# Re-cutting fourteen loads against ScalarE, and twelve unread products ahead of TensorE's last ones

## The chip, the cores and the metric

One core of one Trainium2 chip. The metric is the device time of one execution in microseconds (us), as a median over executions. A "span" is the same execution in the profile, from the first to the last instruction, some 1.8 us shorter than the device time. The experiments ran in four groups on four chips; each group has its own runs of the kernel before, and times are compared inside a group. A run counts as slow when it lies over 1.5% above the fastest of its kernel in the group; medians below are of all runs, ratios of fast runs alone.

## The reference

A cross-entropy loss per row: for 256 rows of 32000 float32 logits, the log of the sum of exponentials, less the logit that the label names.

```python
log_probs = logits - np.max(logits, axis=-1, keepdims=True)
log_probs = log_probs - np.log(np.sum(np.exp(log_probs), axis=-1, keepdims=True))
return np.array([-log_probs[i, labels[i]] for i in range(batch)])
```

## The kernel before

Each of the 128 partitions holds two rows, 64000 columns in one line. They arrive in 14 loads (numbered 0 to 13), all issued by SyncE on one queue. ScalarE runs one exp over each load, which also sums it (two where a load crosses from the first row into the second). The logit of the label is gathered, exp(-g) goes on the diagonal of a matrix, and TensorE multiplies the row sums with it, so that the log of the result is the loss.

```python
CHUNKS = [
    1024, 14528, 13376, 8960, 7168, 5056, 3584,
    2816, 2176, 1536, 1280, 1024, 768, 704,
]
# ... (cut)
for i in range(done, last):
    exps(i)                                   # ScalarE: exp of load i, sum into parts
    if i == turn:                             # first row complete
        nc.vector.reduce_sum(out=sums[:, 0:1], in_=parts[0][:, :], ...)
        nc.tensor.matmul(lane[0][:, :], sums[:, 0:1], diag[0][:, :], start=True, stop=True)
    if i == turn + 1:
        log_row(0)                            # ScalarE: Ln of the first row's products
nc.vector.reduce_sum(out=sums[:, 1:2], in_=parts[1][:, :], ...)
nc.tensor.matmul(lane[1][:, :], sums[:, 1:2], diag[1][:, :], start=True, stop=False)
exps(last)                                    # load 13
nc.tensor.matmul(lane[1][:, :], s_last[:, :], diag[1][:, :], start=False, stop=True)
log_row(1)
nc.sync.dma_start(out=out..., in_=res...)
```

The last three lines are a chain: nothing can start before the last exp's sum is read. Below, "the sums' product" is the first of the two products of row 1, "the last product" the second.

The softmax here doesn't subtract the row's maximum and nothing guards it: scores larger than these inputs give would overflow.

Of the kernel before, what the change touches and what calls it, by code (L numbers as in the profile page):

```python
# [9 lines left out]
P = 128  # L10
ROWS = 2
F32 = mybir.dt.float32
# [3 lines left out]


CHUNKS = [
    1024, 14528, 13376, 8960, 7168, 5056, 3584,
    2816, 2176, 1536, 1280, 1024, 768, 704,  # L20
]
SLOTS = [0, 1, 2, 3, 4, 5, 2]
TAIL = len(SLOTS)
TAIL_SLOT = 1


def begin_first_load_before_barrier(nc):
# [15 lines left out]
@with_exitstack  # L43
def kernel(
    ctx: ExitStack,
    tc: tile.TileContext,
    logits: bass.AP,
    labels: bass.AP,
    out: bass.AP,
):  # L50
    nc = tc.nc
    nc.at_finalize(begin_first_load_before_barrier)
    B, C = logits.shape
    assert B == P * ROWS and sum(CHUNKS) == ROWS * C


    flat = logits.rearrange("(p r) c -> p (r c)", r=ROWS)


    pieces = []  # L60
    starts = []
    at = 0
    for n in CHUNKS:
        starts.append(at)
        cuts = [at] + [c for c in range(C, ROWS * C, C) if at < c < at + n] + [at + n]
        pieces.append([(a, b, a // C) for a, b in zip(cuts, cuts[1:])])
        at += n
    last = len(CHUNKS) - 1

    turn = next(i for i in range(len(CHUNKS)) if starts[i] + CHUNKS[i] >= C)  # L70

    big = ctx.enter_context(tc.tile_pool(name="big", bufs=1))
    small = ctx.enter_context(tc.tile_pool(name="small", bufs=1))
    psum = ctx.enter_context(tc.tile_pool(name="psum", bufs=1, space=bass.MemoryType.PSUM))

    width = {}
    for i, s in enumerate(SLOTS):
        width[s] = max(width.get(s, 0), CHUNKS[i])
    tiles = []
    for i, s in enumerate(SLOTS):  # L80
        tiles.append((big.tile([P, width[s]], F32, name=f"x{i}", tag=f"slot{s}"), starts[i]))
    tail = big.tile([P, width[TAIL_SLOT]], F32, name="x_tail", tag=f"slot{TAIL_SLOT}")
    assert sum(CHUNKS[TAIL:]) <= width[TAIL_SLOT]
    tiles += [(tail, starts[TAIL])] * (len(CHUNKS) - TAIL)

    n_of = [sum(1 for ps in pieces[:-1] for q in ps if q[2] == r) for r in range(ROWS)]
    parts = [small.tile([P, n_of[r]], F32, name=f"parts{r}") for r in range(ROWS)]
    s_last = small.tile([P, 1], F32, name="s_last")
    res = small.tile([1, ROWS * P], F32, name="res")
    sums = small.tile([P, ROWS], F32, name="sums")  # L90
    ident = small.tile([P, P], F32, name="ident")
    diag = [small.tile([P, P], F32, name=f"diag{r}") for r in range(ROWS)]
    lane = [psum.tile([1, P], F32, name=f"lane{r}") for r in range(ROWS)]
    lbl = small.tile([P, 2 * ROWS], I32, name="lbl")
    idx = small.tile([P, ROWS], I32, name="idx")
    g = small.tile([P, ROWS], F32, name="g")
    eg = small.tile([P, ROWS], F32, name="eg")

    nc.scalar.preload_act_table_set("natural_log_exp_and_others")  # L99

    lbl_words = dataclasses.replace(
        labels.tensor, shape=[labels.tensor.shape[0] * 2], dtype=I32
    )

    def load(i):
        t, base = tiles[i]
        a, b = starts[i], starts[i] + CHUNKS[i]
        nc.sync.dma_start(out=t[:, a - base:b - base], in_=flat[:, a:b])  # L108

    seen = [0] * ROWS  # L110

    def exps(i):
        t, base = tiles[i]
        for a, b, r in pieces[i]:
            if i == last:
                acc = s_last[:, :]
            else:
                acc = parts[r][:, seen[r]:seen[r] + 1]
                seen[r] += 1
            nc.scalar.activation(  # L120
                out=t[:, a - base:b - base],
                in_=t[:, a - base:b - base],
                func=AF.Exp,
                accum_out=acc,
            )

    def log_row(r):
        nc.scalar.activation(  # L128
            out=res[0:1, r:ROWS * P:ROWS], in_=lane[r][:, :], func=AF.Ln
        )  # L130

    with tc.manual_schedule():
        first = len(set(SLOTS))
        for i in range(first):
            load(i)

        nc.scalar.dma_start(
            out=lbl[:, :], in_=bass.AP(tensor=lbl_words, offset=0, ap=[[2 * ROWS, P], [1, 2 * ROWS]])
        )
        nc.gpsimd.iota(out=idx[:, :], pattern=[[C, ROWS]], base=0, channel_multiplier=ROWS * C)  # L140
        make_identity(nc, ident[:, :])
        nc.gpsimd.tensor_add(out=idx[:, :], in0=idx[:, :], in1=lbl[:, 0:2 * ROWS:2])  # L142
        for r in range(ROWS):
            nc.gpsimd.indirect_dma_start(  # L144
                out=g[:, r:r + 1],
                out_offset=None,
                in_=logits[:, :],
                in_offset=bass.IndirectOffsetOnAxis(ap=idx[:, r:r + 1], axis=1),
            )


        done = 0
        for i in range(first, len(CHUNKS)):
            slot = SLOTS[i] if i < TAIL else TAIL_SLOT
            while done <= SLOTS[:first].index(slot):
                exps(done)
                done += 1
            load(i)
        nc.scalar.activation(out=eg[:, :], in_=g[:, :], func=AF.Exp, scale=-1.0)  # L159
        for r in range(ROWS):  # L160
            nc.vector.tensor_scalar_mul(diag[r][:, :], ident[:, :], eg[:, r:r + 1])  # L161
        for i in range(done, last):
            exps(i)
            if i == turn:
                nc.vector.reduce_sum(out=sums[:, 0:1], in_=parts[0][:, :], axis=mybir.AxisListType.X)  # L165
                nc.tensor.matmul(lane[0][:, :], sums[:, 0:1], diag[0][:, :], start=True, stop=True)  # L166
            if i == turn + 1:
                log_row(0)
        nc.vector.reduce_sum(out=sums[:, 1:2], in_=parts[1][:, :], axis=mybir.AxisListType.X)  # L169
        nc.tensor.matmul(lane[1][:, :], sums[:, 1:2], diag[1][:, :], start=True, stop=False)  # L170
        exps(last)
        nc.tensor.matmul(lane[1][:, :], s_last[:, :], diag[1][:, :], start=False, stop=True)  # L172
        log_row(1)
        nc.sync.dma_start(
            out=out.rearrange("(a n) -> a n", a=2), in_=res[0:1, :].rearrange("o (a n) -> o a n", a=2)
        )
# [30 lines left out]
```

## Time and profile before

| | before |
|---|---|
| device time, median of 4 runs (lowest to highest) | 84.88 us (84.86 to 84.90) |
| span of the profiled run | 83.03 us |
| ScalarE busy, share of the span | 58.2 us, 70% |
| mean DMA rate | 395 GB/s |
| last load landed / its exp began / its sum was read | 78.95 / 79.17 / 80.04 us |
| ScalarE's wait for the last product | 0.68 us |

"Landed" is when the sixteenth of the sixteen increments of a load's semaphore comes in the trace's landing records. Where the page of the profile gives the same fact, it is the issue's start plus its time to landing.

These are lines of part 5 of the page of the kernel before. The columns are: line, engine, operation, tiles, shapes and count; then busy us and mean ns of one; then the idle time just before the group and what ended it.

```profile
L120 ACT ACTIVATE x<-x 128x1024 f32<-128x1024 f32 (+7 forms) x8 | 46.3, 5786 | 21.3 <-DMA x<-in_logits_dram 21.3
L120 ACT ACTIVATE x_tail<-x_tail 128x2816 f32<-128x2816 f32 (+6 forms) x7 | 9.9, 1412 | 0.0
...
L172 PE MATMUL lane<-diag,s_last 128*1 128x128 f32 x2 | 0.6, 398 | 0.0
```

ScalarE's 21.3 us of idleness lies wholly before the exps of the first loads; the seven tail loads have none. And one product of 128 columns of float32 appears here as two passes of about 398 ns, which overlap: together they last 0.59 us.

### The profile page before, as it was taken

To read this page: it belongs to the slowest core of one execution; us is meant where nothing else is said; L and a number is where in the kernel's file an instruction comes from. 1 tells how busy PE (TensorE), PEld (TensorE's weight loads), DVE (VectorE), ACT (ScalarE), POOL (GpSimd) and SP (SyncE) were. 2 spreads that over 40 slices of the span, in tenths; PEclk is the share of its full clock that TensorE was granted. 3 is DMA by queue.
4 is the path that set the end of the run, shared out by engine and by line. 5 is a ranking of instruction groups with operands and counts; after the bars stand their busy time and mean duration, and the time that the engine had idled before them with its cause. 6 is when DMAs were issued, how large, how long until landed. Compare 5 with 4: busy or idle time off the path is not lost.

```text
span 83.0 us, 126 instructions
## 1 busy us (share of the span) xinstructions
PE 1.7 (2%) x6; PEld 0.3 (0%) x6; DVE 0.8 (1%) x4; ACT 58.2 (70%) x34; POOL 3.0 (4%) x10
## 2 busy tenths in 40 slices
PE   0000000000000000000000002000000000000050
PEld 0000000000000000000000000000000000000000
DVE  0000000000000000000000020000000000000000
ACT  6230000000899999029999999999999999999960
POOL 3000000000640000000000000000000000000000
DMA  4999999999999999979989799999999999999600
GB/s 87 614 448 448 448 448 448 448 448 413 412 412 413 412 413 412 412 328 501 449 380 535 307 401 428 442 451 390 458 411 414 431 434 408 400 415 405 262 0 0
DMA packets 2226, 32.77 MB, mean 395 GB/s; under 512 B 433, under 2 KB 434, under 8 KB 1202
## 3 DMA queue, kind: packets, MB, share of 16 engines
q1 hardware_dynamic: 2018, 32.77, 93.0%
q10 hardware_dynamic: 144, 0.00, 0.1%
q0 software_dynamic: 64, 0.00, 0.1%
HBM read 32.77 MB, written 0.00 MB: 395 GB/s over the span
## 4 chain that ended last, share of the span: by engine, by line
DMA 43%; ACT 37%; issue 14%; PE 1%; SPq 0%; DVE 0%
DMA x<-in_logits_dram 43%; ACT x L120 26%; ACT x_tail L120 11%; PE lane L172 1%; PE lane L170 1%; ACT res L128 1%; SPq L108 0%; DVE sums L169 0%; ACT eg L159 0%
## 5 line engine op out<-in xcount | busy, mean ns | idle before, releaser
L120 ACT ACTIVATE x<-x 128x1024 f32<-128x1024 f32 (+7 forms) x8 | 46.3, 5786 | 21.3 <-DMA x<-in_logits_dram 21.3
L120 ACT ACTIVATE x_tail<-x_tail 128x2816 f32<-128x2816 f32 (+6 forms) x7 | 9.9, 1412 | 0.0
L144 POOL DMA_INDIRECT g<-in_logits_dram,idx x2 | 2.1, 1037 | 0.6 <-issue 0.3
L99 ACT ACT_TABLE_LOAD x1 | 1.3, 1283 | 0.8 <-PEq L191 0.8
L166 PE MATMUL lane<-diag,sums 128*1 128x128 f32 x2 | 0.6, 397 | 51.4 <-DVE sums L165 51.4
L120 ACT ACTIVATION_READ_ACCUMULATOR x<-x 128x1 f32 x8 | 1.5, 186 | 0.0
L120 ACT ACTIVATION_READ_ACCUMULATOR x_tail<-x_tail 128x1 f32 x7 | 1.3, 185 | 0.0
L170 PE MATMUL lane<-diag,sums 128*1 128x128 f32 x2 | 0.6, 397 | 27.5 <-DVE sums L169 27.5
L128 ACT ACTIVATE res<-lane 1x128 f32<-1x128 f32 x2 | 0.5, 266 | 0.7 <-PE lane L172 0.7
L161 DVE TENSOR_SCALAR diag<-ident,eg 128x128 f32<-128x128 f32 x2 | 0.5, 285 | 48.5 <-ACT eg L159 48.5
L142 POOL TENSOR_TENSOR idx<-idx,lbl 128x2 int32<-128x2 int32 x1 | 0.2, 193 | 19.6 <-DMA lbl<-in_labels_dram 19.6
L172 PE MATMUL lane<-diag,s_last 128*1 128x128 f32 x2 | 0.6, 398 | 0.0
L169 DVE TENSOR_REDUCE sums<-parts 128x1 f32<-128x10 f32 x1 | 0.2, 164 | 27.9 <-ACT x_tail L120 27.9
masks.py:199 POOL TENSOR_SCALAR_AFFINE_SELECT ident<-ident 128x128 f32<-128x128 f32 x1 | 0.3, 292 | 0.1
L166 PEld LDWEIGHTS lane<-diag,sums 128*1 128x1 f32 x2 | 0.1, 80 | 51.4 <-DVE sums L165 51.4
masks.py:197 POOL MEMSET ident<- 128x128 f32 x1 | 0.2, 194 | 0.0
L159 ACT ACTIVATE eg<-g 128x2 f32<-128x2 f32 x1 | 0.2, 187 | 0.0
L165 DVE TENSOR_REDUCE sums<-parts 128x1 f32<-128x4 f32 x1 | 0.2, 157 | 2.2 <-ACT x L120 2.2
L170 PEld LDWEIGHTS lane<-diag,sums 128*1 128x1 f32 x2 | 0.1, 80 | 28.0 <-DVE sums L169 28.0
L140 POOL IOTA idx<- 128x2 int32 x1 | 0.1, 120 | 0.5 <-POOLq L191 0.5
L191 POOL MEMSET const-uint8-127<- 128x1 uint8 x1 | 0.1, 118 | 0.0
L191 POOL MEMSET const-bfloat16-1.0<- 128x1 bf16 x1 | 0.1, 112 | 0.0
(3 smaller groups left out, 0.3 us busy)
## 6 DMA issues: line engine op xcount, KB each, us to landing
x<-in_logits_dram SPq DMA_DIRECT2D x1, 7264.0 KB, 20.1
x<-in_logits_dram SPq DMA_DIRECT2D x1, 6688.0 KB, 35.7
x<-in_logits_dram SPq DMA_DIRECT2D x1, 4480.0 KB, 45.8
x<-in_logits_dram SPq DMA_DIRECT2D x1, 3584.0 KB, 53.9
x<-in_logits_dram SPq DMA_DIRECT2D x1, 2528.0 KB, 59.3
x<-in_logits_dram SPq DMA_DIRECT2D x1, 1792.0 KB
x_tail<-in_logits_dram SPq DMA_DIRECT2D x1, 1408.0 KB, 21.0
x_tail<-in_logits_dram SPq DMA_DIRECT2D x1, 1088.0 KB, 23.1
```

Of the source, the lines that this page charges most:

```text
L99: nc.scalar.preload_act_table_set("natural_log_exp_and_others")
L120: nc.scalar.activation(out=t[:, a - base:b - base], in_=t[:, a - base:b - base], func=AF.Exp, accum_out=acc,)
L128: nc.scalar.activation(out=res[0:1, r:ROWS * P:ROWS], in_=lane[r][:, :], func=AF.Ln)
L142: nc.gpsimd.tensor_add(out=idx[:, :], in0=idx[:, :], in1=lbl[:, 0:2 * ROWS:2])
L144: nc.gpsimd.indirect_dma_start(out=g[:, r:r + 1], out_offset=None, in_=logits[:, :], in_offset=bass.IndirectOffsetOnAxis(ap=idx[:, r:r + 1 ...
L159: nc.scalar.activation(out=eg[:, :], in_=g[:, :], func=AF.Exp, scale=-1.0)
L161: nc.vector.tensor_scalar_mul(diag[r][:, :], ident[:, :], eg[:, r:r + 1])
L165: nc.vector.reduce_sum(out=sums[:, 0:1], in_=parts[0][:, :], axis=mybir.AxisListType.X)
L166: nc.tensor.matmul(lane[0][:, :], sums[:, 0:1], diag[0][:, :], start=True, stop=True)
L169: nc.vector.reduce_sum(out=sums[:, 1:2], in_=parts[1][:, :], axis=mybir.AxisListType.X)
L170: nc.tensor.matmul(lane[1][:, :], sums[:, 1:2], diag[1][:, :], start=True, stop=False)
L172: nc.tensor.matmul(lane[1][:, :], s_last[:, :], diag[1][:, :], start=False, stop=True)
```

## The change

The intent is two-fold. The loads are cut anew, so that ScalarE, which in the profile of before works a column off faster than the DMA brings it (0.83 ns, from 12309 ns for 14528 columns and 772 for 704, against 1.19, from 15.92 us between landings for 13376 columns), has some slack in each step. And TensorE, idle for 27.5 us since the first row's products, is given twelve products whose result nobody reads, so that its clock is up when the last two products come. That this would raise it was an assumption; the result below shows it, with passes 109 to 110 ns apart in place of 213 to 214.

```diff
 CHUNKS = [
-    1024, 14528, 13376, 8960, 7168, 5056, 3584,
-    2816, 2176, 1536, 1280, 1024, 768, 704,
+    1024, 15104, 12672, 8960, 7136, 4992, 3872,
+    2848, 2144, 1600, 1216, 992, 800, 640,
 ]
+WARM_FROM = 8
+WARM = 12
...
+    warm = psum.tile([1, P], F32, name="warm")
...
             if i == turn + 1:
                 log_row(0)
+            if i == WARM_FROM:
+                col = parts[1][:, seen[1] - 1:seen[1]]
+                for _ in range(WARM):
+                    nc.tensor.matmul(warm[:, :], col, diag[0][:, :], start=True, stop=True)
```

The products read the sum of load 8, so that they can't begin before it is there.

## The prediction

Its sum was 84.87 less 0.18 for the sizes and 0.21 for the products, 84.48. The 0.18 is worked out from the profile of before. The 0.21 is its author's estimate: that a risen clock brings the product from 0.59 to 0.38 us was not shown by that profile. The upper figure for a risen clock, 84.51, holds a charge of 0.03 us for loads that start off 256 B.

> **What bounds the kernel now.** I read the chain that ended last first, then the loads' times to landing, then the last five microseconds instruction by instruction.
>
> The busy shares and the chain:
>
> ```profile
> PE 1.7 (2%) x6; PEld 0.3 (0%) x6; DVE 0.8 (1%) x4; ACT 58.2 (70%) x34; POOL 3.0 (4%) x10
> DMA 43%; ACT 37%; issue 14%; PE 1%; SPq 0%; DVE 0%
> ```
>
> Two things share the span. The DMA moves 32.77 MB (its row of tenths reads 9 nearly throughout), and ScalarE computes exp over the same 64000 columns. The chain in order of time shows the hand-over:
>
> ```profile
> 1.19 35.68 DMA x<-in_logits_dram
> 36.87 0.02 issue
> 36.90 0.03 ACT x L120
> ```
>
> Until 36.87 us the chain is the DMA, landing loads 0, 1 and 2; from 36.90 it is ScalarE. So the sum that sets the end today is the landing of load 2, then all the exp of loads 2 to 13 without a gap, then a tail. The same shows in ScalarE's wait on the DMA, 3 times and never after load 2:
>
> ```profile
> L120 ACT ACTIVATE x<-x 128x13376 f32<-128x13376 f32 x1 | 11.3, 11349 | 3.5 <-DMA x<-in_logits_dram 3.5
> L120 ACT ACTIVATE x_tail<-x_tail 128x704 f32<-128x704 f32 x1 | 0.8, 772 | 0.0
> ```
>
> How near the DMA runs behind is the question that decides this change. A load's landing is its issue's start plus its time to landing:
>
> ```profile
> x_tail<-in_logits_dram SPq DMA_DIRECT2D x1, 352.0 KB, 16.9
> ```
>
> The SyncE timeline puts that last issue at 62.04, so it lands at about 78.95. ScalarE starts on it at 79.17, which is 0.22 late. The landing records of the trace (sixteenth increment of each load's semaphore) give for loads 3 to 13: 47.50, 56.00, 62.02, 66.32, 69.71, 72.34, 74.23, 75.82, 77.09, 78.08, 78.95. The exps start at 48.34, 56.17, 62.49, 66.89, 70.06, 72.59, 74.59, 76.06, 77.31, 78.34, 79.17. ScalarE is thus 0.17 to 0.84 us behind each landing. It is the bound, but only by that much; if it were earlier, the DMA would be.
>
> The tail:
>
> ```profile
> 79.17 0.77 ACT L120 ACTIVATE x_tail<-x_tail 128x704 f32<-128x704 f32 x1
> 79.30 0.16 DVE L169 TENSOR_REDUCE sums<-parts 128x1 f32<-128x10 f32 x1 [27.93 <-ACT x_tail L120]
> 79.51 0.59 PE L170 MATMUL lane<-diag,sums 128*1 128x128 f32 x2 [27.50 <-DVE sums L169]
> 79.85 0.19 ACT L120 ACTIVATION_READ_ACCUMULATOR x_tail<-x_tail 128x1 f32 x1
> 80.09 0.59 PE L172 MATMUL lane<-diag,s_last 128*1 128x128 f32 x2
> 80.71 0.27 ACT L128 ACTIVATE res<-lane 1x128 f32<-1x128 f32 x1 [0.68 <-PE lane L172]
> 81.01 0.32 SPq L174 DMA_DIRECT2D out_dram<-res  x1
> ```
>
> The last accumulator read ends at 80.04, one product of two passes fills 0.59, ScalarE waits 0.68 for it, then Ln and the store, about 2.3 us that the change leaves alone.
>
> [...] 704 columns took 772 ns, 14528 took 12309. With the accumulator read I find start to start 0.833 n + 0.183 us (2816 columns: 70.06 to 72.59, 2.53).
>
> [...] TensorE here idles 27.5 us before its tail products[...]. The trace has only modelled ends, 374 ns for the first pass, 0.59 for both: 214 ns between the two ends[...]. The profile's granted clock says 1.00 throughout[...].
>
> [...] All starts of before are multiples of 64 columns (256 B)[...].
>
> **The change part by part.** *Sizes.* Same 64000 columns, same 14 loads, same 15 exp pieces, so bytes, descriptors and instruction counts stand. The DMA's end should stay at 78.95: it runs saturated, and a load costs about 1.19 ns a column between landings (load 1 to 2: 15.92 us for 13376 columns) with a little per load on top. I interpolate the new landings on the old ones by cumulative column. Loads 1 to 13 then land at 21.64, 36.72, 47.35, 55.81, 61.75, 66.40, 69.83, 72.42, 74.39, 75.90, 77.13, 78.16, 78.95.
>
> Now ScalarE against these, with 0.025 us from landing to start. Load 2 starts at 36.74, 0.15 earlier, and has 704 columns less, 0.59 us. It ends at 47.49, and the exp of the gathered labels follows to 47.59. Load 3 in its two pieces (3200 and 5760 columns) ends at 55.42. Load 4 lands only at 55.81, so ScalarE waits 0.42: the bound changes to the DMA here. Load 4 runs from 55.84 to 61.97, the first row's Ln takes 0.16, load 5 starts at 62.12, load 6 at 66.47, load 7 at 69.88. From there each starts within 0.1 us of its landing: 72.44, 74.41, 75.93, 77.16, 78.18, and the last at 79.03, against 79.17 (the same arithmetic run on the old sizes gives 79.14, a check to 0.03). Last start: 0.11 earlier by model against model. Last piece: 64 columns fewer, 0.05. Model against model the last accumulator read ends 0.16 earlier; against the measured 80.04 it is 79.84, 0.20. I take **0.18 us** gained.
>
> *Products.* Twelve products are added after load 8's exp, which ends at 74.4 and whose accumulator is read by 74.50. Each is two passes at 214 ns while cold, 0.43 us: twelve are 5.1 us, 74.55 to 79.67 if the clock never rises. [...] The sums' product L170 is ready when load 12's accumulator (79.12), the reduction (0.16) and two hand-overs are done, at 79.36. [...] cold ones delay L170 by 0.3. The last product L172 can start 0.05 after the last accumulator read, 79.89. [...] 0.59 becomes 0.38, **0.21 us** gained on the path. ScalarE's wait would fall from 0.68 to 0.47. The products wait for ScalarE, not the reverse, nothing reads their PSUM tile, and 10240 tail columns fit the slot of 15104: no new wait on ScalarE or the loads.
>
> *Sum:* 0.18 + 0.21 = 0.39; 84.87 − 0.39 = 84.48.
>
> **The rivals.** *The clock does not rise in time.* [...] If cold, the warm-up ends at 79.67, L170 runs to 80.10, and L172 starts there, where it started before (80.09): the earlier ScalarE is given back too, and the time is 84.87. That is the largest uncertainty; I give the rise in time 65%.
>
> *The sizes lose at the DMA.* Loads 5, 6, 8 and 12 of the new set start on 128 B, not on 256. [...]
>
> *ScalarE stays the bound.* From load 2 on it has 576 columns less (load 1 took them while ScalarE waited anyway), 0.48 us, and starts 0.15 earlier. Then all 0.63 us would come through, 84.03 with the clock. Against it stand the landings: the slack was 0.17 at load 4 and 0.22 at the last, and a faster ScalarE can't pass them.
>
> *The products disturb the tail.* Were a pass longer in a stream than 214 ns (each also loads weights, 80 ns in the trace, begun beside the pass before), the twelve could run to 80 or beyond and cost up to 1 us. The starts of two weight loads 3 ns apart in L172 speak against it.
>
> **Range and chances.** Clock risen (65%): 84.48 to 84.51, give or take 0.08. Not risen: 84.80 to 84.90, little changed. Most weight is at the first, so I predict 84.5 us, with 84.35 to 84.86 to hold it 8 times in 10. Two per cent is 1.7 us; nothing I found gains or loses that, so faster 0.01, within 2% 0.98, slower 0.01.
>
> **What would show it.** The step of sizes is right if ScalarE waits some 0.4 us for the DMA at 7136 columns and for some small loads after, and starts the last load near 79.0; wrong if the last load lands later than 78.97 or ScalarE never waits after load 2. The step of products is right if the later of the 24 passes are about half as far apart as the first and ScalarE's wait before the last Ln is 0.45 to 0.50; wrong if it stays 0.68, or if L170 starts only when the twelve are done.

## The result, and the profile after

| | before | changed |
|---|---|---|
| device time, median of 4 runs (lowest to highest) | 84.88 (84.86 to 84.90) | 84.41 (84.30 to 84.60) |
| span of the profiled run | 83.03 | 82.55 |
| load 2 landed, its exp began | 36.87, 36.90 | 36.70, 36.72 |
| last load landed, its exp began | 78.95, 79.17 | 78.71, 78.95 |
| last sum read | 80.04 | 79.76 |
| ScalarE's wait for the last product | 0.68 | 0.47 |

The ratio is 0.9947 (95% interval 0.9927 to 0.9966). Ratios here are the mean time of one kernel's fast runs over that of the other's of the same rounds, so not quite the ratio of the medians. In this group the change is faster by half a per cent, clear of noise and far under 2%. Two later groups repeat the pair on other chips, with more scatter: there the ratio is 0.9954 with an interval that holds 1, and 1.0018.

Part 5 of the page of the changed kernel, the groups that answer to those of before:

```profile
L124 ACT ACTIVATE x<-x 128x1024 f32<-128x1024 f32 (+7 forms) x8 | 46.4, 5794 | 20.9 <-DMA x<-in_logits_dram 20.9
L124 ACT ACTIVATE x_tail<-x_tail 128x2848 f32<-128x2848 f32 (+6 forms) x7 | 9.8, 1404 | 0.0
L176 PE MATMUL warm<-diag,parts 128*1 128x128 f32 x24 | 4.7, 382 | 23.2 <-ACT x_tail L124 23.2
...
L180 PE MATMUL lane<-diag,s_last 128*1 128x128 f32 x2 | 0.4, 270 | 0.1
```

The last product's two passes took 270 ns each where they took 398. The 24 added passes have a mean between (382): most were slow, the last few fast. By their starts in the trace, they follow each other by 213 to 214 ns from the second pass on until 78.31 us, then once by 190, and from 78.50 on by 109 to 110. The tail loads still never made ScalarE wait.

The last microseconds, by the timeline (start, length, engine, line, operation; in brackets the idle time before it and what ended it):

```profile
74.52 4.69 PE L176 MATMUL warm<-diag,parts 128*1 128x128 f32 x24 [23.16 <-ACT x_tail L124]
...
78.95 0.72 ACT L124 ACTIVATE x_tail<-x_tail 128x640 f32<-128x640 f32 x1
79.08 0.16 DVE L177 TENSOR_REDUCE sums<-parts 128x1 f32<-128x10 f32 x1 [28.37 <-ACT x_tail L124]
...
79.29 0.38 PE L178 MATMUL lane<-diag,sums 128*1 128x128 f32 x2
79.58 0.18 ACT L124 ACTIVATION_READ_ACCUMULATOR x_tail<-x_tail 128x1 f32 x1
...
79.81 0.38 PE L180 MATMUL lane<-diag,s_last 128*1 128x128 f32 x2
80.23 0.27 ACT L132 ACTIVATE res<-lane 1x128 f32<-1x128 f32 x1 [0.47 <-PE lane L180]
```

The warm-up ends at 74.52 + 4.69 = 79.21, before the sums' product is ready at 79.29, so it delays nothing. The last product lasts 0.38 us, and the bracket on the Ln reads 0.47.

The chain in order of time shows where ScalarE took over from the DMA:

```profile
36.72 0.02 ACT x L124
...
55.51 0.25 another core or an unknown queue
55.75 0.02 issue
55.78 6.24 ACT x L124 x2
```

The "unknown queue" is the landing of load 4, which the landing records put at 55.75. From 55.78 on the chain is ScalarE without a gap, up to the last product. So the bound is the DMA up to load 4, and then ScalarE again, not the DMA.

The mean granted clock of this run is 0.996 although TensorE ran slow for most of it. The trace has clock records only from the first change on: one at 78.47 us, full, for 3.413 us, and one at 81.88, half. What lies before the first record counts as full: half the clock lost from 81.88 to 82.55, over 82.55 us, is the 0.004 that is missing. The matmul spacing is the thing to read here.

### The profile page after: what moved, and what is told of

It reads as the page before. It is cut to its first block, busy times and chain, and to the rows that moved or that the text cites. A ratio compares the mean times of both kernels' runs of the same rounds, so it can differ in the third digit from the quotient of the medians.

```text
span 82.6 us, 174 instructions
## 1 busy us (share of the span) xinstructions
PE 6.0 (7%) x30; PEld 2.9 (4%) x30; DVE 0.8 (1%) x4; ACT 58.4 (71%) x34; POOL 3.0 (4%) x10
## 4 chain that ended last, share of the span: by engine, by line
DMA 43%; ACT 39%; issue 13%; PE 0%; SPq 0%; another core or an unknown queue 0%
DMA x<-in_logits_dram 43%; ACT x L124 27%; ACT x_tail L124 12%; ACT res L132 1%; PE lane L180 0%; SPq L112 0%; ACT eg L163 0%
## 5 line engine op out<-in xcount | busy, mean ns | idle before, releaser
L124 ACT ACTIVATE x_tail<-x_tail 128x2848 f32<-128x2848 f32 (+6 forms) x7 | 9.8, 1404 | 0.0
L176 PE MATMUL warm<-diag,parts 128*1 128x128 f32 x24 | 4.7, 382 | 23.2 <-ACT x_tail L124 23.2
L176 PEld LDWEIGHTS warm<-diag,parts 128*1 128x1 f32 x24 | 2.7, 115 | 25.4 <-ACT x_tail L124 23.7
```

The lines of the kernel that those rows point to most:

```text
L124: nc.scalar.activation(out=t[:, a - base:b - base], in_=t[:, a - base:b - base], func=AF.Exp, accum_out=acc,)
L176: nc.tensor.matmul(warm[:, :], col, diag[0][:, :], start=True, stop=True)
```

## The experiments

Two measures are used that a late DMA in the first loads doesn't disturb. One is the stretch from the start of the exp of load 2 to the read of the last sum; the other is ScalarE's wait for the last product. Device times are given beside them.

**The sizes alone.** The changed kernel without the products.

```diff
-WARM = 12
+WARM = 0
```

> The new sizes alone, no added products. Theory (the two parts are independent and add): ScalarE runs as in the changed kernel, waits about 0.27 us for load 4, starts the last load near 78.95; its wait for the last product stays 0.68, as in the kernel before; time 84.60, 0.27 less than before. Rival (the rise of the clock carries the whole gain, the earlier ScalarE came from a faster run of the DMA in that one profile): last accumulator read near 80.0 and time 84.80 or more.

Measured: median 84.70 us (84.56 to 85.25, 6 runs) against 84.86 (84.72 to 85.55, 11 runs) for the kernel before of the group; ratio 0.9987, interval 0.9948 to 1.0026. On time alone this settles nothing; the chip scatters by almost a per cent. The profile of its 84.56 us run settles it.

```profile
78.97 0.72 ACT L124 ACTIVATE x_tail<-x_tail 128x640 f32<-128x640 f32 x1
...
79.59 0.19 ACT L124 ACTIVATION_READ_ACCUMULATOR x_tail<-x_tail 128x1 f32 x1
...
79.83 0.59 PE L180 MATMUL lane<-diag,s_last 128*1 128x128 f32 x2
80.46 0.27 ACT L132 ACTIVATE res<-lane 1x128 f32<-1x128 f32 x1 [0.68 <-PE lane L180]
```

The last sum is read at 79.78, as in the changed kernel (79.76), and the last product is slow, as before. The span is 82.77, 0.35 under the 83.12 of the kernel before on the same chip. In the profile the theory's numbers hold; the gain in time isn't shown.

**The products alone.** The old sizes with the new products.

```diff
-    1024, 15104, 12672, 8960, 7136, 4992, 3872,
-    2848, 2144, 1600, 1216, 992, 800, 640,
+    1024, 14528, 13376, 8960, 7168, 5056, 3584,
+    2816, 2176, 1536, 1280, 1024, 768, 704,
```

> The old sizes with the twelve products. Theory: gain 0.21 us by the clock where it rises before the last product: 84.66; where it doesn't, the products end about 79.8, push the sums' product to there and the last one to 80.23: about 85.0. Single runs then scatter from 84.6 to 85.0, where the kernel before scatters by 0.04. Rival (a rise a fixed 4.0 us after the first product): every run 84.66 within 0.05.

Measured: median 84.70 us (84.52 to 85.02, 6 runs), ratio 0.9977 (0.9941 to 1.0013). In the profile the wait is 0.47, the span 82.92, 0.20 under the 83.12 of the kernel before on the same chip:

```profile
79.94 0.19 ACT L124 ACTIVATION_READ_ACCUMULATOR x_tail<-x_tail 128x1 f32 x1
...
80.60 0.27 ACT L132 ACTIVATE res<-lane 1x128 f32<-1x128 f32 x1 [0.47 <-PE lane L180]
```

With the sizes' 0.35 that makes 0.55, against 0.48 for both on the first chip (83.03 to 82.55); the spans also hold how late the first loads were. The two measures that leave those out show that the parts are independent: the stretch is 43.14 us with the old sizes and 43.04 with the new, with and without products, and the wait is 0.68 without products and 0.47 with them, for both sets of sizes. The scatter of single runs is no evidence for a missed rise, though, since the kernel before scattered as much in this group.

**Six products.**

```diff
-WARM = 12
+WARM = 6
```

> New sizes, six products in place of twelve: 2.6 us of cold work. Theory [...]: the clock never rises, the passes stay 213 ns apart, ScalarE's last wait is 0.68, the time is that of the sizes alone, 84.60, without scatter. Rival [...]: a rise in some runs, ScalarE's last wait 0.47, single runs near 84.4.

Measured: median 84.59 us (84.37 to 85.01, 6 runs), ratio 0.9962 (0.9925 to 1.0000). In the profile the twelve added passes stay 213 to 214 ns apart from the second on, and the wait is that of a slow product, 0.67:

```profile
74.70 2.72 PE L176 MATMUL warm<-diag,parts 128*1 128x128 f32 x12 [23.16 <-ACT x_tail L124]
...
80.62 0.27 ACT L132 ACTIVATE res<-lane 1x128 f32<-1x128 f32 x1 [0.67 <-PE lane L180]
```

But one of the other runs, the fastest (84.37), reports a mean clock of 0.992. In the changed kernel's profile a mean under 1 (0.996) came with a rise at 78.47 and a fall at 81.88. If it is so here, six products (2.72 us of passes in the profile above) sufficed in that run, and the theory that the clock never rises with six is in doubt. By an estimate, a loss of 0.008 of 82.6 us at half clock puts the fall about 1.3 us before the end, at 81.3; if the clock was up for 3.413 us, as in the changed kernel, it rose at 77.9. That is worked out from a rounded mean, not seen in a trace.

**The kernel before, again.**

> The kernel before, unchanged, for a second profile. It asks whether the last load's landing (78.95 in the first profile, 78.71 in the changed kernel) belongs to the sizes or to the run. Theory (it is the run): the landing in this profile differs from 78.95 by 0.1 us or more, or the changed sizes elsewhere land near 78.95. Rival (the sizes make the DMA end earlier): 78.95 again within 0.05. Time 84.88 either way, since ScalarE sets it.

Measured: median 84.88 us (84.73 to 85.24, 6 runs). The last load landed at 79.02, and at 79.01 in the products-alone kernel; with the new sizes it was 78.71, 78.71 and 78.86. Between the landings of loads 3 and 13 lie 31.45, 31.45 and 31.43 us with the old sizes, 31.39, 31.38 and 31.37 with the new, which have 128 columns more in that stretch, worth 0.15. So my theory fell: the earlier landing belongs to the sizes, some 0.2 us of it, and not to the run.

**The changed kernel, again.**

> The changed kernel again, as the yardstick of this group and for more single runs. Theory [...]: its runs scatter more than the kernel before's, in runs with a rise before the last product (ScalarE's last wait 0.47) and runs without; median 0.4 to 0.5 us under before. Rival (the rise follows the first product by a fixed time): no more scatter than the kernel before. Last landing 78.7 again.

This group ran on a chip with more scatter: the kernel before took 84.76 to 86.64, six of its eleven runs slow. Measured: median 85.01 (84.42 to 86.91, 6 runs, two of them slow), ratio 0.9954 (0.9877 to 1.0030). In the profile the last landing is 79.18, not 78.7. The landing records show why: load 1's first engine was done at 21.06, its last at 22.08, 1.0 us apart where the first profile had 0.44, and every later load carries that. The stretch from load 2's exp to the last sum is 43.04 us, as in the first profile, and the wait 0.47. So the later end of this run comes from one or more late DMA engines within load 1, not from TensorE's clock, and the expectation that the rise makes the scatter can't be read from times. The runs over 86 us weren't profiled; that they have the same cause isn't shown. Nor was the kernel before profiled on this chip or the later ones, so whether its load 1 has engines as late isn't known; its times were slow more often (6 of 11 against 2 of 6). The clock rose at 79.61, 4.6 us after the first product; in the first profile it was 3.95. So the delay wasn't the same in these two runs.

**Sixteen products, begun a load earlier.**

```diff
-WARM_FROM = 8
-WARM = 12
+WARM_FROM = 7
+WARM = 16
```

> Sixteen products from load 7's exp on (72.4 us) in place of twelve from load 8's (74.5): 6.8 us of cold work[...]. Theory: a rise in every run, all runs as the changed kernel's good ones, median 0.5 us or more under before. Rival (an early rise is lost again when the products end early[...]): part of the runs have the last product cold and lie 0.2 us higher, so no better than twelve.

Measured: median 85.21 (84.35 to 87.16, 6 runs), ratio 0.9987 (0.9905 to 1.0069): nothing gained that can be told. The profile, of the 84.35 us run, is worth more than the time:

```profile
72.55 5.08 PE L176 MATMUL warm<-diag,parts 128*1 128x128 f32 x32 [21.18 <-ACT x_tail L124]
79.30 0.38 PE L178 MATMUL lane<-diag,sums 128*1 128x128 f32 x2 [1.67 <-DVE sums L177]
79.82 0.38 PE L180 MATMUL lane<-diag,s_last 128*1 128x128 f32 x2
```

The clock record rises at 75.51, 2.96 us after the first product, where it was 3.95 and 4.6 in the two profiles of the changed kernel so far. In the profile of the next experiment the clock rose at 79.84, 4.83 us after the first product at 75.01, and in the look with the widened tile, further down, at 79.43, 4.95 us after the one at 74.48. So the rise came 2.96 to 4.95 us after the first product in these five profiles, and in the one with six products, 2.72 us of passes, it did not come. What sets the moment isn't shown.

The products ended early, with 1.67 us idle after them, and the clock stayed up: the last two products took 0.38 us each. So the rival wasn't met in this profile. By an estimate from the run's rounded mean clock, 0.999 over 82.6 us, the fall at half clock came near 82.4, some 6.9 us after the rise; in the first profile of the changed kernel it was 3.41 us (78.47 to 81.88). So the clock doesn't stay up for the same time in every run either; what decides it isn't shown.

**224 columns from load 4 to load 5.**

```diff
-    1024, 15104, 12672, 8960, 7136, 4992, 3872,
+    1024, 15104, 12672, 8960, 6912, 5216, 3872,
```

> The changed kernel with 224 columns moved from load 4 to load 5 (6912 and 5216). In the changed kernel ScalarE waits 0.27 us for load 4 and never again, and starts the last load 0.24 after its landing. Theory: load 4 lands at about 55.48, the wait there is gone, and the last load starts near 78.83 in place of 78.95: 0.1 us faster. Rival (the wait only moves to load 5, or the last landing is the bound): last start 78.95 or later, no gain.

Measured: median 84.99 (84.63 to 86.31, 6 runs), ratio 0.9992 (0.9912 to 1.0071); the stretch from load 2's exp to the last sum is 43.02, in place of 43.04. The expected 0.1 us didn't come. ScalarE began load 4 0.22 after its last read began in place of 0.46, so 0.24 was saved there. But then loads 5 and 6 made ScalarE wait (it began them 0.02 and 0.08 after they landed): the steps to them took 0.08 and 0.12 us longer than in the changed kernel, so that 0.20 of the 0.24 was lost again. The rival was right: the wait moved on.

**Every load on a multiple of 64 columns.**

```diff
-    1024, 15104, 12672, 8960, 7136, 4992, 3872,
-    2848, 2144, 1600, 1216, 992, 800, 640,
+    1024, 15104, 12672, 8960, 7168, 4992, 3840,
+    2816, 2176, 1600, 1216, 1024, 768, 640,
```

A packet is one entry of the trace's record of the DMA; each load has 128 of them, with four bytes for each of its columns. The "fixed cost" or "fixed part" of a packet, below, is an estimate of what is left of its time when its bytes, at one rate, are taken off. For instance, in the changed kernel packets of 19968 B took 742.1 ns in the mean and those of 11392 B 427.1, so 315 ns for 8576 B; at that rate 9 ns are left of the former, and 12.5 of the 332.2 ns that packets of 8704 B took in the kernel before. What these nanoseconds are isn't shown.

> The changed kernel with sizes rounded so that every load starts on a multiple of 64 columns (256 B): 7168, 4992, 3840, 2816, 2176, 1600, 1216, 1024, 768, 640. The new sizes' last load landed at 78.71 to 78.86 in three profiles and the old ones' at 78.95 to 79.02 in three. Theory one [...]: landing earlier than 78.7. Theory two (a fixed cost of a packet goes with its own size; 8 to 10 ns for the new sizes, 12 to 14 for the old): the sizes shared with before (7168, 2816, 2176, 1024, 768) show 12 to 14, the rest 8 to 10, and the landing is about 78.85. Theory three (it is a matter of place, not size): all 8 to 10, landing 78.7. Time within 0.1 of the changed kernel.

Measured: median 84.98 (84.53 to 87.52, 6 runs), ratio 0.9978 (0.9886 to 1.0069). Between the landings of loads 3 and 13 lie 31.56 us, against 31.34 to 31.42 for the same number of columns with the changed kernel's sizes (the run of the 224 columns has the 31.42). The *aligned* starts were slower by about 0.2 us, and the stretch of ScalarE grew with them, to 43.13 from 43.04. Theory one, by which these starts would let the last load land earlier, is refuted. Theory two fits some sizes (a packet of 8704 B took 333 ns, as before), but not those taken over from the changed kernel: packets of 19968 B took 745 ns here and 742 there. So size isn't it.

**Every start off by 128 B, and the tiles alone off by 128 B.** Two looks. The first moves 32 columns from the last load to the first; the second leaves the sizes and widens the first tile by 32 unused columns, which moves the tiles behind it.

```diff
 # off by 128 B, in memory and in the tiles
-    1024, 15104, 12672, 8960, 7168, 4992, 3840,
-    2816, 2176, 1600, 1216, 1024, 768, 640,
+    1056, 15104, 12672, 8960, 7168, 4992, 3840,
+    2816, 2176, 1600, 1216, 1024, 768, 608,
 # the tiles alone (rounded sizes kept)
     width[s] = max(width.get(s, 0), CHUNKS[i])
+    width[0] += 32
```

> The rounded sizes with 32 columns moved from the last load to the first (1056 and 608): every load after the first now starts 128 B off a 256 B boundary, in memory and in the tiles. With every start on 256 B the landings of loads 3 to 13 lay 31.56 us apart; with the changed kernel's mixed starts 31.34 to 31.39 for the same columns. Theory (a load that starts or ends off 256 B is the cheaper one here): 31.52 by the columns alone becomes about 31.3 and the fixed part of a packet falls from 12 to 9 ns in all loads. Rival (the gain needs single sizes, not the offset): 31.5 and 12 ns.

> The rounded sizes, with the first tile 32 columns wider than its load: the tiles behind it lie 128 B further on in SBUF, the addresses in memory stay on 256 B. Theory (the place in memory decides): 31.56 us between the landings of loads 3 and 13, as with the rounded sizes. Rival (the place in SBUF decides): about 31.35.

Measured: 31.23 us from landing to landing for the first, 31.24 for the second; times 84.69 and 84.30, one run each (the kernel before beside them: 86.10, one run). The packets of 8704 B took 328 ns in both. That speaks for the rival of the second look, the place in SBUF: with the tiles moved by 128 B the DMA took 0.32 us less (31.24 against 31.56). The 31.56 is from another chip, and on this one the rounded sizes weren't profiled without the shift. Two things speak against the chip as the cause: with the changed kernel's sizes it was 31.34 to 31.39 in six profiles on at least three chips, and the next chip was profiled with both placements, where packets of 4864 B, of a load that starts on 256 B in memory both times, took 189.8 ns in the mean in the changed kernel and 187.0 in the kernel with the widened tile, as on this chip. In the first look, memory starts were off 256 B as well and cost nothing that can be seen: 31.23 plus 0.04 for the 32 columns fewer, against 31.24. The tiles' true addresses aren't in the trace, so which of the two placements is the aligned one stays open.

It didn't make ScalarE earlier: in the second look the last load landed at 78.50 and ScalarE began it at 78.92, 0.41 late. The changed kernel is bound by ScalarE after load 4 (its last load was begun 0.24 after its landing), and the faster DMA of this look only lengthened the queue.

**A kernel built on these.** Load 2 is cut down so that ScalarE works while load 3 is under way, in place of waiting 2.3 us for load 2; the rest is spread so that it meets each landing.

```diff
-    1024, 15104, 12672, 8960, 7136, 4992, 3872,
-    2848, 2144, 1600, 1216, 992, 800, 640,
+    1024, 14464, 4544, 11968, 8576, 6336, 4544,
+    3456, 2560, 1984, 1536, 1216, 960, 832,
...
-WARM = 12
+WARM = 13
...
+        width[0] += 32
```

> A kernel built on what the runs showed: the first tile 32 columns wider (earlier landings), load 2 cut from 12672 to 4544 columns so that ScalarE doesn't idle after load 1, the other sizes chosen so that ScalarE meets each landing with under 0.15 us of slack, loads 0 to 3 ending on the row's end (one exp fewer), thirteen products from load 8 on. Theory: where no engine is late, the last load lands at about 78.4, ScalarE starts it within 0.1 us, the last accumulator read ends at 79.3 (79.76 in the changed kernel), its wait is 0.47; 83.9 us, or 0.5 us under the changed kernel of the same group. Rival (a load this size early changes the DMA's pace or ScalarE falls behind elsewhere): the last start over 0.2 behind the landing, no gain over the changed kernel.

> The changed kernel once more, as the yardstick for the other kernel of this group: 0.4 to 0.5 us under before (ratio about 0.995), its last accumulator read 43.04 us after its exp of load 2 begins, last wait 0.47.

Measured on a fourth chip: the built kernel 84.78 (84.15 to 85.64, 6 runs), ratio to before 0.9913 (0.9833 to 0.9992); the changed kernel 85.42 (85.19 to 85.80, 6 runs), ratio 1.0018 (0.9968 to 1.0068); before 85.56 (84.89 to 87.29, 11 runs). The changed kernel's gain isn't to be seen in this group: in its profile the engines of load 1 were 1.4 us apart and the last sum came at 80.69, while its stretch (43.05) and its wait (0.47) were as ever. The built kernel's profile:

```profile
33.19 3.97 ACT L125 ACTIVATE x<-x 128x4544 f32<-128x4544 f32 x1
...
40.59 10.18 ACT L125 ACTIVATE x<-x 128x11968 f32<-128x11968 f32 x1 [3.24 <-DMA x<-in_logits_dram]
...
78.74 0.88 ACT L125 ACTIVATE x_tail<-x_tail 128x832 f32<-128x832 f32 x1
...
80.18 0.27 ACT L133 ACTIVATE res<-lane 1x128 f32<-1x128 f32 x1 [0.47 <-PE lane L181]
```

Load 2's exp follows load 1's without a gap, and the last load, landed at 78.69, is begun 0.05 later: ScalarE is no longer behind. The last sum is read at 79.71. The 79.3 worked out for it did not come (the changed kernel's first profile has 79.76): the last load landed 0.3 later than worked out. Against the changed kernel of its own group it was 0.75% faster in the medians (85.42 to 84.78), or 1.1% by the means of the fast runs (85.44, 6 runs, to 84.50, 4 runs), but the intervals of the two ratios overlap, and the late engines of load 1 fall as they will. I take it as likely, not as settled. Sizes, products and the widened tile changed together here, so the gain isn't split among them.

## Why the prediction was right or wrong

**The sum.** Predicted 84.5, range 84.35 to 84.86, within 2%; measured 84.41. The gain of 0.39 was 0.47 by the medians; by the profile, the term of the products came out to the hundredth, and that of the sizes was 0.09 short. That the total came out so near owes something to a quiet group, in which the kernel before scattered by 0.04 us; in the later group with the ratio 1.0018, where the engines of load 1 were 1.4 us apart, it would not have.

**The sizes, 0.18 us.** The last sum was read 0.27 earlier (80.04 to 79.76). The mechanism was mostly as told: load 2's exp began 0.18 earlier (0.15 foretold), load 4 made ScalarE wait (its read began at 55.32, the next exp 0.46 later, where back to back is 0.09; 0.42 of waiting had been foretold by the model, 0.37 came), and 576 columns fewer from load 2 on were worth 0.48. From load 2's exp to the last sum that leaves 0.48 less 0.37, 0.11; measured 0.10 (43.14 to 43.04).

**The step that failed inside it** is "the DMA's end should stay at 78.95". It landed at 78.71. So the waits foretold for the small loads never came: ScalarE began the last load 0.24 behind its landing. The prediction had the bound pass to the DMA for good at load 4; it passed back. The term was mis-sized for this reason: the landings worked out were up to 0.24 late, and with them the waits and the last start, 79.03 where 78.95 was measured. The prediction had 31.60 us from the landing of load 3 to the last, where 31.39 was measured; with the sizes rounded to multiples of 64 columns, as all sizes of the kernel before are, it was 31.56. The looks with the moved tiles point to the cause: with the tiles 128 B further on in SBUF, the same loads 4 to 13 took 0.32 us less (31.24). For the changed kernel's own mix of places that is an inference. Nothing in the profile of before told it.

**The rival of starts off 256 B** had the wrong sign. The sizes with some starts off the boundary were the faster ones (31.34 to 31.42 us against 31.56), and in the first look starts off it in memory showed no cost that could be seen (31.27 with the 0.04, against 31.24). The rival "ScalarE stays the bound", argued away by the landings, came nearer than I allowed: after load 4 it was the bound. Its 84.03 failed, because load 4's wait ate most of the 0.48.

**The products, 0.21 us.** The wait fell from 0.677 to 0.469, 0.208. Passes fell from 213 to 109 ns apart. The profile of before shows the two ends 214 ns apart; that they would come half as far apart was an assumption, which the changed kernel then showed. The clock column reads 1.00 over the slow products of before, a trace without clock records; the changed kernel's record has the rise at 78.47.

**The chance that the clock rises in time, 65%,** looks too low: in all eight profiles with twelve products the wait was 0.47, and in the two with more. In the changed kernel the last product starts 5.30 us after the first added one, and in the five profiles listed above the rise came 2.96 to 4.95 us after the first. Eight of eight don't settle what the chance is. In three of those profiles the rise came late (79.43, 79.61 and 79.84) and the warm-up ended after the sums' product was ready, which began 0.25, 0.06 and 0.19 us late; the last product wasn't delayed, since it waits for the last sum anyway.

**What stays open:** what sets the moment at which the clock rises (2.96 to 4.95 us after the first product) and how long it stays up, and why a packet took 3 to 5 ns less with the tiles moved (187.0 against 189.8, and 328 against 333).

## What to carry to other kernels

Where two engines run within a quarter of a microsecond of each other, list each landing beside the start of its work: the gain of a re-cut is the lesser of two slacks, and a wait removed at one load can turn up at the next (of 0.24 us saved at load 4, 0.20 came back at loads 5 and 6). A product at the very end of an idle TensorE was made shorter here, 0.38 us in place of 0.59, by unread products placed so that they are done when the last ones come. And on a noisy chip a stretch inside one profile tells a tenth of a microsecond that a median of six runs can't.
